# A gate vector computed on the array instead of in the network's loop, and a fixed order on ScalarE, in a two-layer diffusion trunk

## The chip, the cores and the metric

The kernel runs on one core of a Trainium2 chip. The metric is the device time of one execution in microseconds (us); lower is better. Engines are named as in the profile: PE is TensorE (matrix products and transposes), DVE is VectorE, ACT is ScalarE, SP is the queue that issues nearly all transfers.

## What is computed

Two token groups, 128 context tokens and 256 latent tokens (three blocks of 128 tokens, b = 0, 1, 2), go through two layers of one shared trunk. Cut to what matters here:

```
mod = silu(cond) @ w_mod[l] + b_mod[l]
sh1, sc1, g1, sh2, sc2, g2 = split(mod, 6)
u = layer_norm(x) * (1 + sc1) + sh1
h = mixer(u)
x = layer_norm(ALPHA * x + g1 * h)
u = layer_norm(x) * (1 + sc2) + sh2
x = layer_norm(ALPHA * x + g2 * ((silu(u @ w_gate) * (u @ w_up)) @ w_down))
```

`cond` is one vector per token group. Each of the six modulation vectors of a layer is a product of two condition vectors with a 1024 x 1024 piece of `w_mod`. Vector 5 of a layer, `g2`, is the gate of the feed-forward network ("the network" below). It is needed only when the network's output is added to `x`.

## The kernel before, in words

Weights arrive as f32 tiles of 512 KB in a ring of five buffers (tag "raw", `raw_unit`, L162). `split` (L172) makes two tiles of each: a rounded copy by ACT (L173) and the rest by DVE (L175). They go to rings of five buffers ("wr" and "wl"). A product is then three matmul passes (`in_block`, L378, and `proj`, L524).

Between the mixer and the network stands `w_out_phase`, once per layer. The string `WORDER[l]` writes out the order in which its steps are traced:

- `P b` (`project`): the output projection of block b in two halves of 512 columns, 24 matmuls each, then the residual on DVE (L358, L359), the mean (L297) and the square sum on ACT (L298, tile `junk`).
- `A b`: DVE's chain of small operations for the inverse root (L189 to L201), two DVE operations that finish x (L366), the next mean (L297) and the second square sum on ACT (L298, tile `so`).
- `B b`: the same chain, then the normalised block, by ACT (L313) for blocks 0 and 1, by DVE (L311) for block 2.
- `F b` (`to_u`, `make_u_half`): in two halves, four PE transposes (tile `puo`), four scaled copies (L330, tile `ufo`), the rounded copy on ACT (L333, tile `urf`) and the rest on DVE (L334, tile `ulf`).
- `G`, `U`: load and split two units each of the first 256 columns of `w_gate` and `w_up`.
- `H b` (`head`): the products of block b with these columns (`hg`, then `hu`), silu by ACT (L484, tile `hsg`), their product on DVE (L487), two transposes. Their banks come from a pool of two (`psA`).
- `X`: from here on DVE's part of each split is queued behind block 2's last `ulf` (`gate`). `M`: products of vectors listed in `WMODS`, which is empty.

The order of a step string is not yet the order on the engines. The framework's scheduler plays the program forward with times of its own and gives each engine what is ready, earlier traced first; `boost` raises an instruction, and `tc.issue_after(ins)` puts what is traced inside it behind `ins` on the same engine (order only, no wait for its end). The order that comes out is fixed in the program: each engine then works through its own queue.

The network (`ffn_phase`) runs over ten column pairs: gate product, silu, a piece of the down product, up product, another piece. Between them `steps` advances a generator (`all_mods`, `mod_steps`) over the vectors in `SMODS[l]`, `MSTEPS` = (3, 2) steps per pair. One step loads 512 KB of `w_mod` (tile `mraw`) and multiplies it by a column of the conditions into two row sums `z`: with ACT for the first of eight (L247), with DVE for the other seven (L250), once per condition. After eight steps 16 PE passes with a column of ones sum over partitions (L255). In layer 0 six vectors go this way, with (0, 5), the gate of layer 0's network, first; in layer 1 one.

The other way is `mod_now` with `mod_pe` (L223 to L235): each of the eight 512 KB tiles (`rawm`) goes through the "raw" ring and straight into PE against 32 columns, four products of 256 columns per tile, eight PE passes in the trace (L118 when boosted). Layer 0's mixer uses `mod_pe` for three vectors.

Of the kernel before, what the change touches and what calls it, by code (L numbers as in the profile page):

```python
# [19 lines left out]
P = 128  # L20
# [8 lines left out]
WMODS = ((), ())  # L29
TMODS = ()  # L30
SMODS = (((0, 5), (1, 1), (1, 0), (1, 3), (1, 4), (1, 2)), ((1, 5),))
# [6 lines left out]
WORDER = ("P0 P1 G A0 B0 F0 A1 B1 P2 U H0 F1 A2 B2 F2 X H1 M H2", "G P0 P1 A0 B0 A1 B1 U P2 F0 F1 H0 A2 B2 F2 X H1 M H2")  # L38
# [4 lines left out]
MSTEPS = (3, 2)  # L43
# [21 lines left out]
def trunk_kernel(ctx: ExitStack, tc: tile.TileContext, a: dict):  # L65
# [101 lines left out]
    gate = [None]  # L167

    def gated():
        return tc.issue_after(gate[0].ins) if gate[0] is not None else nullcontext()  # L170

    def split(t, r, lo):  # L172
        S.copy(r, t)  # L173
        with gated():
            V.tensor_tensor(lo, t, r, ALU.subtract)  # L175
        return r, lo
# [60 lines left out]
    def mod_steps(l, v, out):  # L237
# [3 lines left out]
        for k in range(KC):  # L241
            t = big([P, D], f"mraw{l}_{v}_{k}")
            SY.dma_start(t, w[:, k, v * D : (v + 1) * D])
            for c in range(2):
                if k == 0:
                    with gated():
                        S.mul(z[c], t, cs[:, c, k : k + 1])  # L247
                else:
                    with gated():
                        V.scalar_tensor_tensor(z[c], t, cs[:, c, k : k + 1], z[c], ALU.mult, ALU.add)  # L250
            yield k == KC - 1
# [43 lines left out]
    def acc_stats(src, junk, sums, name):  # L295
        w = perm.tile([P, 8], F32, tag="lnw", name="lnw" + name, bufs=NLNW)
        V.tensor_scalar(w[:, 0:1], sums[:, 0:1], sums[:, 1:2], -1.0 / D, ALU.add, ALU.mult)  # L297
        S.activation(junk, src, AF.Square, bias=w[:, 0:1], accum_out=w[:, 1:2])  # L298
        return w
# [6 lines left out]
    def make_xh(x, xh, w, name, fast=False):  # L306
        rs = var_rsqrt(w, name)
        nmr = w[:, 2:3]
        last = V.tensor_scalar(nmr, w[:, 0:1], rs, None, ALU.mult)
        if fast:  # L310
            V.tensor_scalar(xh, x, rs, nmr, ALU.mult, ALU.add)  # L311
        else:
            S.activation(xh, x, AF.Identity, bias=nmr, scale=rs)  # L313
        return last

    def make_u_half(b, xh, uf, sh, sc, u, bank, name, hb, fast=False):
# [4 lines left out]
        for q in range(4):  # L321
            k = hb * 4 + q
            boost(nc.tensor.transpose, pt[:, q * P : (q + 1) * P], xh[:, k * P : (k + 1) * P], ident)
# [9 lines left out]
        S.copy(ur[:, ks, cols], uf)  # L333
# [101 lines left out]
    def w_out_phase(l, pre, cat, x, gt, lnv, u2, sh2, sc2, wx, hh, bankTO, mods):  # L435
# [4 lines left out]
        units2, st = {}, {}  # L440

        def head_units(nm, src):
            v = src[l].rearrange("(k p) f -> p k f", p=P)
            units2[nm] = []
            for i in range(2):
                r, lo = split_unit(v[:, 4 * i : 4 * i + 4, 0:256], [4, 256], f"{nm}h{l}_{i}")
                units2[nm].append((r, lo, 4, 4 * i))

        def project(b):
            s = big([P, D], f"so{l}_{b}")  # L450
            sums = small([P, 2], "rsum")
            for nh in range(2):
                ps = bk("V" if (b, nh) == (1, 1) else "W", f"wo{l}_{nh}_{b}")
                in_block(ps, cat, units[nh], b, 512)
# [9 lines left out]
        def to_u(b):  # L464
            tags = iter((None, "WV", "WW")[b] or ())
            bank = bankTO if b == 0 else lambda nm: bk(next(tags), nm)
            last[b] = make_u(b, st[b][0], sh2, sc2, u2, f"o{l}_{b}", bank, b == 2)

        def mod_all():
            for ll, v in mods:  # L470
                mod_now(ll, v, bk("W", f"mw{ll}_{v}"))

        def hold_splits():
            gate[0] = last[2]

        heads = []

        def head(b):
# [5 lines left out]
            S.activation(sg, ps[:, 0:256], AF.Silu)  # L484
# [5 lines left out]
        def head_end(b, sg):  # L490
            pt = bankTO(f"ht{l}_{b}")
            for q in range(NHEAD):
# [4 lines left out]
                              "G": lambda: head_units("g", a["w_gate"]), "U": lambda: head_units("u", a["w_up"]),  # L497
                              "M": mod_all, "X": hold_splits})
# [6 lines left out]
    def ffn_phase(l, u2, x, lnp, hh, wx_es, pto, get_g, lnv, steps, keep, late, tail_units, tail_block, tail_mod, end_heads):  # L505
# [89 lines left out]
        gate[0] = None  # L595
# [37 lines left out]
        gate[0] = None  # L633
# [723 lines left out]
    for l in range(2):  # L1357
# [34 lines left out]
        end_heads = w_out_phase(l, pre, cat, x, gt, lnv, u2, m[l, 3], m[l, 4], wx, hh, bankTO, WMODS[l])  # L1392
# [135 lines left out]
```

## Time and profile before

| what | value |
|---|---|
| median of 3 runs | 1015.73 us (1014.62 to 1015.8) |
| the profiled execution's own time | 1014.2 us |
| its span in the profile | 1012.4 us |
| PE busy | 984.8 us (97%) |
| DVE busy | 667.7 us (66%) |
| ACT busy | 436.6 us (43%) |
| read from HBM | 167.52 MB, 170 GB/s over the span |
| granted PE clock | 0.998 of full speed |

The profile records one execution. The span goes from the first to the last recorded instruction; the execution's own time is 1.8 us longer. Busy time of PE counts matmuls whose ends are modelled. Idle time of an engine costs the kernel something only where the engine that bounds the stretch waits for it.

### The profile page before, as it was taken

What the parts mean: (1) busy time and instruction counts of PE and PEld (TensorE: products, weight loads), DVE (VectorE), ACT (ScalarE), POOL (GpSimd) and SP (SyncE); (2) the same over time, 40 slices, a digit from 0 to 9 for tenths busy, and PEclk for the clock granted to TensorE, in tenths of its full rate; (3) what the DMA queues carried; (4) which work ended last, traced back from release to release, by engine and by line L of the source; (5) the groups of instructions that cost most, each with busy time, mean ns of one, the idle gap of its engine ahead of it and who ended that gap; (6) DMA issues with size and microseconds to landing.
All of it is one profiled execution on the core that took longest, in us unless ns stands there. A gap on an engine that the chain in (4) does not pass through costs nothing.

```text
span 1012.4 us, 14717 instructions
## 1 busy us (share of the span) xinstructions
PE 984.8 (97%) x5583; PEld 824.2 (81%) x5583; DVE 667.7 (66%) x1368; ACT 436.6 (43%) x790; POOL 1.2 (0%) x5
## 2 busy tenths in 40 slices
PE   9999999999999999999999999999899999999996
PEld 4775567787899988989887766787799999999985
DVE  5387558588875877968788577558895333335554
ACT  3385533227533343334327555544943333333410
POOL 0000000000000000000000000000000000000000
PEclk9999999999999999999999999999999999999999
DMA  9975446473674877767754333235574544444401
GB/s 304 296 205 188 147 133 205 174 254 111 195 230 137 281 224 249 219 216 227 253 163 153 99 95 94 84 104 225 163 246 153 163 126 126 124 126 124 149 22 42
DMA packets 109704, 172.85 MB, mean 171 GB/s; under 512 B 10177, under 2 KB 78273, under 8 KB 109633
## 3 DMA queue, kind: packets, MB, share of 16 engines
q1 hardware_dynamic: 106960, 170.87, 53.0%
q10 hardware_dynamic: 2672, 1.04, 0.4%
q8 instruction: 44, 0.72, 0.3%
q14 instruction: 28, 0.22, 0.1%
HBM read 167.52 MB, written 4.36 MB: 170 GB/s over the span
## 4 chain that ended last, share of the span: by engine, by line
PE 81%; DVE 6%; ACT 6%; DMA 5%; issue 2%; SPq 0%; ACTq 0%; DVEq 0%
PE dn L544 18%; PE wg L524 15%; PE wu L524 14%; PE cd L378 7%; PE wo L378 4%; PE rvg L378 4%; PE s L378 3%; PE rqk L378 2%; PE mod L118 1%; DMA mraw<-in_w_mod 1%; DMA rawm<-in_w_mod 1%; DMA raw_wd<-in_w_down 1%; PE ms L118 1%; PE hg L378 1%; ACT ufo L330 1%
## 5 line engine op out<-in xcount | busy, mean ns | idle before, releaser
L250 DVE SCALAR_TENSOR_TENSOR z<-mraw,cs,z 128x1024 f32<-128x1024 f32 x98 | 121.5, 1281 | 12.2 <-DMA mraw<-in_w_mod 11.8
L524 PE MATMUL wu<-urf,r_wu 128*128 128x384 f32 x320 | 108.6, 340 | 1.2 <-ACT sg L565 1.2
L524 PE MATMUL wg<-urf,r_wg 128*128 128x384 f32 x320 | 108.2, 340 | 0.4 <-DVE sg L572 0.4
L524 PE MATMUL wu<-ulf,r_wu 128*128 128x384 f32 x320 | 108.3, 338 | 0.0
L524 PE MATMUL wg<-ulf,r_wg 128*128 128x384 f32 x320 | 108.2, 338 | 0.0
L524 PE MATMUL wg<-urf,l_wg 128*128 128x384 f32 x320 | 108.1, 338 | 0.0
L524 PE MATMUL wu<-urf,l_wu 128*128 128x384 f32 x320 | 108.0, 338 | 0.0
L175 DVE TENSOR_TENSOR l_wg<-raw_wg,r_wg 128x1024 fp32r<-128x1024 f32 x40 | 48.8, 1223 | 56.6 <-ACT r_wg L173 56.6
L173 ACT CAST r_wd<-raw_wd 128x1024 fp32r<-128x1024 f32 x36 | 37.8, 1050 | 94.5 <-PE wu L524 44.2
L175 DVE TENSOR_TENSOR l_wd<-raw_wd,r_wd 128x1024 fp32r<-128x1024 f32 x36 | 44.0, 1222 | 47.9 <-ACT r_wd L173 47.9
L173 ACT CAST r_wg<-raw_wg 128x1024 fp32r<-128x1024 f32 x40 | 42.0, 1050 | 74.3 <-PE dn L544 28.5
L175 DVE TENSOR_TENSOR l_wu<-raw_wu,r_wu 128x1024 fp32r<-128x1024 f32 x40 | 48.5, 1223 | 35.0 <-ACT r_wu L173 35.0
L173 ACT CAST r_wu<-raw_wu 128x1024 fp32r<-128x1024 f32 x40 | 42.0, 1050 | 57.6 <-issue 18.9
L544 PE MATMUL dn<-l_wd,hr 128*128 128x512 f32 x168 | 66.6, 396 | 0.0
L544 PE MATMUL dn<-r_wd,hr 128*128 128x512 f32 x168 | 66.5, 396 | 0.0
L544 PE MATMUL dn<-r_wd,hl 128*128 128x512 f32 x168 | 66.5, 396 | 0.0
L524 PEld LDWEIGHTS wu<-urf,r_wu 128*128 128x128 f32 x320 | 60.1, 188 | 3.6 <-ACT sg L565 2.0
L524 PEld LDWEIGHTS wg<-urf,r_wg 128*128 128x128 f32 x320 | 60.1, 188 | 2.6 <-issue 1.2
L524 PEld LDWEIGHTS wu<-ulf,r_wu 128*128 128x128 f32 x320 | 60.1, 188 | 0.5
L524 PEld LDWEIGHTS wg<-ulf,r_wg 128*128 128x128 f32 x320 | 60.1, 188 | 0.4
L524 PEld LDWEIGHTS wu<-urf,l_wu 128*128 128x128 f32 x320 | 60.1, 188 | 0.1
L524 PEld LDWEIGHTS wg<-urf,l_wg 128*128 128x128 f32 x320 | 60.1, 188 | 0.0
(415 smaller groups left out, 2163.9 us busy)
## 6 DMA issues: line engine op xcount, KB each, us to landing
mraw<-in_w_mod SPq DMA_DIRECT2D x56, 512.0 KB
raw_wd<-in_w_down SPq DMA_DIRECT2D x44, 512.0 KB
raw_wg<-in_w_gate SPq DMA_DIRECT2D x40, 512.0 KB
raw_wu<-in_w_up SPq DMA_DIRECT2D x40, 512.0 KB
rawm<-in_w_mod SPq DMA_DIRECT2D x24, 512.0 KB
raw_cd<-in_w_in_cd SPq DMA_DIRECT2D x20, 512.0 KB
ms<-in_w_mod SPq DMA_DIRECT2D x16, 512.0 KB
raw_rqk<-in_w_in_ab SPq DMA_DIRECT2D x16, 256.0 KB
```

Of the source, the lines that this page charges most:

```text
L118: return f(*args, **kw)
L173: S.copy(r, t)
L175: V.tensor_tensor(lo, t, r, ALU.subtract)
L250: V.scalar_tensor_tensor(z[c], t, cs[:, c, k : k + 1], z[c], ALU.mult, ALU.add)
L330: S.activation(uf[:, q, :], pt[:, q * P : (q + 1) * P], AF.Identity, bias=sh[:, c, k : k + 1], scale=sc[:, c, k : k + 1])
L378: op = mm(ps[:, col : col + width], u[pu][:, k0 + kk, b * P : (b + 1) * P], (r, lo)[pw][:, kk, :], start=(first and i == 0 and pu + pw == ...
L524: mm(ps[j][:, 0:NTOK], un[i][pw][:, k, j * P : (j + 1) * P], u2[pu][:, 4 * i + k, :], start=(i == 0 and k == 0 and pu + pw == 0), stop=(i ...
L544: mm(acc[b, nh], h[fc][ph][:, b * P : (b + 1) * P], wrl[pw][:, nh * 512 : (nh + 1) * 512], start=(fc == 0 and ph + pw == 0), stop=(last an ...
```

## The change

1. Vector (0, 5) leaves `SMODS[0]`, so five vectors stay in layer 0's network loop, and `MSTEPS` goes from (3, 2) to (2, 2). It is computed by `mod_now(0, 5, ...)` in step `M` of layer 0, traced between `H1` and `H2`, with a bank of the pool of two that the head blocks use.
2. `G` and `U` are traced one unit at a time. In both layers the order becomes `A0 B0 A1 B1 Y G1 U0 U1 F0 P2 F1 H0 ...` after `P0 P1`.
3. A new step `Y` records block 1's normalised copy on ACT (L313) as `gate_s`: the rounded copies of splits traced after it are queued behind it on ACT. `Y` also traces one silu of a single column, boosted, behind that copy.
4. `F0`'s ACT instructions are queued behind the last split's rounded copy traced before (that of `U1`). The second half of `P2` is queued on PE behind `F0`'s last transpose; the transposes of `F1` and `F2` behind `P2`.
5. The silu of a head block is queued behind the last `urf` copy traced before: `F1`'s for `H0`, `F2`'s for `H1`.
6. At `X`, `gate_s` becomes `F2`'s last `urf` copy: splits and the first row products of a vector (L247) traced after it are queued behind it.

```diff
-WMODS = ((), ())
-SMODS = (((0, 5), (1, 1), (1, 0), (1, 3), (1, 4), (1, 2)), ((1, 5),))
+SMODS = (((1, 1), (1, 0), (1, 3), (1, 4), (1, 2)), ((1, 5),))
...
-WORDER = ("P0 P1 G A0 B0 F0 A1 B1 P2 U H0 F1 A2 B2 F2 X H1 M H2", "G P0 P1 A0 B0 A1 B1 U P2 F0 F1 H0 A2 B2 F2 X H1 M H2")
+WORDER = ("P0 P1 G0 A0 B0 A1 B1 Y G1 U0 U1 F0 P2 F1 H0 A2 B2 F2 X H1 M H2", "G0 P0 P1 A0 B0 A1 B1 Y G1 U0 U1 F0 P2 F1 H0 A2 B2 F2 X H1 H2")
...
-MSTEPS = (3, 2)
+MSTEPS = (2, 2)
...
-    gate = [None]
-    def gated():
-        return tc.issue_after(gate[0].ins) if gate[0] is not None else nullcontext()
+    gate, gate_s = [None], [None]
+    last_s, last_split, last_t = [None], [None], [None]
+    def gated(g=gate):
+        return tc.issue_after(g[0].ins) if g[0] is not None else nullcontext()
     def split(t, r, lo):
-        S.copy(r, t)
+        with gated(gate_s):
+            last_split[0] = S.copy(r, t)
...
                 if k == 0:
-                    with gated():
+                    with gated(gate_s):
                         S.mul(z[c], t, cs[:, c, k : k + 1])
...
-            S.activation(xh, x, AF.Identity, bias=nmr, scale=rs)
+            last_s[0] = S.activation(xh, x, AF.Identity, bias=nmr, scale=rs)
...
-        S.copy(ur[:, ks, cols], uf)
+        last_s[0] = S.copy(ur[:, ks, cols], uf)
...
             for nh in range(2):
                 ps = bk("V" if (b, nh) == (1, 1) else "W", f"wo{l}_{nh}_{b}")
-                in_block(ps, cat, units[nh], b, 512)
+                with tc.issue_after(last_t[0].ins) if (b, nh) == (2, 1) else nullcontext():
+                    last_p2[0] = in_block(ps, cat, units[nh], b, 512)
...
-            last[b] = make_u(b, st[b][0], sh2, sc2, u2, f"o{l}_{b}", bank, b == 2)
-        def mod_all():
-            for ll, v in mods:
-                mod_now(ll, v, bk("W", f"mw{ll}_{v}"))
+            with tc.issue_after((last_split, last_p2, last_p2)[b][0].ins):
+                last[b] = make_u(b, st[b][0], sh2, sc2, u2, f"o{l}_{b}", bank, b == 2)
+        def gate_vector():
+            mod_now(0, 5, bankA("mw"))
+        def after_norms():
+            gate_s[0] = last_s[0]
+            tiny = small([P, 1], "silu")
+            with gated(gate_s):
+                boost(S.activation, tiny, ones[:, 0:1], AF.Silu)
         def hold_splits():
             gate[0] = last[2]
+            gate_s[0] = last_s[0]
...
-            S.activation(sg, ps[:, 0:256], AF.Silu)
+            with tc.issue_after(last_s[0].ins):
+                S.activation(sg, ps[:, 0:256], AF.Silu)
...
-        gate[0] = None
+        gate[0] = gate_s[0] = None
```

## Rows read from the trace of the kernel before

**Rows 1.** The page's first part: busy us, share of the span, instructions of each engine

```profile
PE 984.8 (97%) x5583; PEld 824.2 (81%) x5583; DVE 667.7 (66%) x1368; ACT 436.6 (43%) x790; POOL 1.2 (0%) x5
```

**Rows 2.** Windows, core 0: PE, PEld, DVE, ACT, POOL busy; granted clock; DMA share; GB/s

```profile
243.00:269.00 26.00, 22.13 (x170) 20.38 (x169) 20.03 (x56) 20.42 (x40) 0.00 (x0) 1.00 0.45 141
269.00:480.00 211.00, 211.00 (x1154) 194.92 (x1153) 163.58 (x168) 77.37 (x93) 0.00 (x0) 1.00 0.71 227
480.00:530.00 50.00, 48.13 (x268) 42.38 (x268) 42.26 (x62) 15.81 (x21) 0.00 (x0) 1.00 0.65 205
712.00:741.00 29.00, 26.15 (x194) 24.02 (x193) 24.34 (x62) 24.84 (x46) 0.00 (x0) 1.00 0.49 156
```

**Rows 3.** Timeline of PE: start, length, instruction, [idle before it <- what ended that]

```profile
516.40 1.07 PE L255 MATMUL mod<-z,ones 128*32 128x256 f32 x16 [0.69 <-DVE sg L572]
717.88 0.38 PE L378 MATMUL hg<-r_gh,ulf 128*128 128x256 f32 x1 [0.93 <-DVE ulf L334]
726.33 0.39 PE L378 MATMUL hg<-r_gh,urf 128*128 128x256 f32 x1 [1.35 <-ACT hsg L484]
```

**Rows 4.** Timeline of ACT, layer 0, around head block 0

```profile
247.65 2.21 ACT L247 ACTIVATE z<-mraw,cs 128x1024 f32<-128x1024 f32 x2
249.88 1.28 ACT L484 ACT_TABLE_LOAD   x1
251.17 0.38 ACT L484 ACTIVATE hsg<-hg 128x256 f32<-128x256 f32 x1
```

**Rows 5.** Chain that ended last, in order of time, layer 1: projection, last head block, network

```profile
693.95 10.49 PE wo L378 x45
737.32 2.85 PE hu L378 x24
740.17 8.45 PE wg L524 x48
```

**Rows 6.** Timeline of DVE, layer 1: residual, mean, one chain, finishing x

```profile
700.43 0.75 DVE L366 SCALAR_TENSOR_TENSOR x<-x,lnwao,lnv 128x512 f32<-128x512 f32 x1
704.46 0.69 DVE L358 TENSOR_TENSOR so<-wo,g 128x512 f32<-128x512 f32 x1 [2.59 <-PE wo L378]
705.91 0.21 DVE L297 TENSOR_SCALAR lnwao<-rsum 128x1 f32<-128x1 f32 x1
717.14 0.68 DVE L334 TENSOR_TENSOR ulf<-ufo,urf 128x512 fp32r<-128x512 f32 x1
727.96 0.15 DVE L189 TENSOR_SCALAR lnwbo<-lnwbo 128x1 f32<-128x1 f32 x1 [0.45 <-ACT so L298]
729.48 0.81 DVE L311 TENSOR_SCALAR so<-x,lnwbo 128x1024 f32<-128x1024 f32 x1
```

**Rows 7.** Timeline of ACT, layer 1, from block 1's square sum to `F0`

```profile
706.57 1.15 ACT L298 ACTIVATE junk<-so,lnwao 128x1024 bf16<-128x1024 f32 x1
708.85 1.99 ACT L173 CAST r_uh<-raw_uh 128x1024 fp32r<-128x1024 f32 x2
711.78 1.25 ACT L313 ACTIVATE so<-x,lnwbo 128x1024 f32<-128x1024 f32 x1
714.06 1.83 ACT L330 ACTIVATE ufo<-puo,modc,modc 128x128 f32<-128x128 f32 x5
715.78 0.62 ACT L333 CAST urf<-ufo 128x512 fp32r<-128x512 f32 x1
```

**Rows 8.** Timeline of PE: eight transposes; two tiles of a vector by `mod_pe` back to back

```profile
718.22 1.04 PE L118 MATMUL puo<-ident,so 128*128 128x128 f32 x8
90.82 1.18 PE L118 MATMUL mod<-rawm,cmod 128*32 128x256 f32 x16
```

**Rows 9.** Timeline of SP, layer 0: the last tile loaded ahead of the head blocks

```profile
222.59 0.38 SPq L164 DMA_DIRECT2D raw_wg<-in_w_gate  x1
```

**Rows 10.** Groups by line: the row products on DVE

```profile
L250 DVE SCALAR_TENSOR_TENSOR z<-mraw,cs,z 128x1024 f32<-128x1024 f32 x98 | 121.5, 1281 | 12.2 <-DMA mraw<-in_w_mod 11.8
```

**Rows 11.** Windows, the last stretch, columns as in rows 2

```profile
1005.00:1012.00 7.00, 0.00 (x0) 0.00 (x0) 4.08 (x15) 1.24 (x2) 0.00 (x0) 0.68 0.20 75
```

More of the change, by code (lines that the diff above doesn't have):

```diff
@@ L297, in acc_stats @@
         V.tensor_scalar(w[:, 0:1], sums[:, 0:1], sums[:, 1:2], -1.0 / D, ALU.add, ALU.mult)
-        S.activation(junk, src, AF.Square, bias=w[:, 0:1], accum_out=w[:, 1:2])
+        last_s[0] = S.activation(junk, src, AF.Square, bias=w[:, 0:1], accum_out=w[:, 1:2])
         return w
@@ L322, in make_u_half @@
             k = hb * 4 + q
-            boost(nc.tensor.transpose, pt[:, q * P : (q + 1) * P], xh[:, k * P : (k + 1) * P], ident)
+            last_t[0] = boost(nc.tensor.transpose, pt[:, q * P : (q + 1) * P], xh[:, k * P : (k + 1) * P], ident)
         for q in range(4):
@@ L433, in wo_unit, with w_out_phase @@
         return r, lo, 2, 2 * i
-    def w_out_phase(l, pre, cat, x, gt, lnv, u2, sh2, sc2, wx, hh, bankTO, mods):
+    def w_out_phase(l, pre, cat, x, gt, lnv, u2, sh2, sc2, wx, hh, bankTO):
         bk = Banks(f"pw{l}", W=3, V=1)
@@ L439, in w_out_phase, with head_unit @@
         units[1] = pre + [wo_unit(l, 1, i, extra_rl(wx, nx, f"{l}{i}")) for i in KORDER[l][len(pre) :]]
-        units2, st = {}, {}
-        def head_units(nm, src):
+        units2, st, last_p2 = {}, {}, [None]
+        def head_unit(nm, src, i):
             v = src[l].rearrange("(k p) f -> p k f", p=P)
[L444 to L447, printed above, removed]
+            r, lo = split_unit(v[:, 4 * i : 4 * i + 4, 0:256], [4, 256], f"{nm}h{l}_{i}")
+            units2.setdefault(nm, []).append((r, lo, 4, 4 * i))
         def project(b):
@@ L496, in w_out_phase @@
         run_order(WORDER[l], {"P": project, "A": norm, "B": norm, "F": to_u, "H": head,
-                              "G": lambda: head_units("g", a["w_gate"]), "U": lambda: head_units("u", a["w_up"]),
-                              "M": mod_all, "X": hold_splits})
+                              "G": lambda i: head_unit("g", a["w_gate"], i), "U": lambda i: head_unit("u", a["w_up"], i),
+                              "Y": after_norms, "M": gate_vector, "X": hold_splits})
         bk.close()
@@ L632, in ffn_phase @@
                 keep(b, x[b])
-        gate[0] = None
+        gate[0] = gate_s[0] = None
         accp.close()
@@ L1391, in trunk_kernel @@
         hh = tuple(lnp.tile([P, NHEAD, NTOK], F32R, name=f"hh{q}{l}") for q in "rl")
-        end_heads = w_out_phase(l, pre, cat, x, gt, lnv, u2, m[l, 3], m[l, 4], wx, hh, bankTO, WMODS[l])
+        end_heads = w_out_phase(l, pre, cat, x, gt, lnv, u2, m[l, 3], m[l, 4], wx, hh, bankTO)
         if wxr_es is not None:
```

## The prediction, made before the changed kernel ran

> **What bounds the kernel now.** I read the page's busy times first [rows 1]: PE is busy for 984.8 us of a span of 1012.4 us. A change can therefore gain by two things only, fewer PE passes or less of the 27.6 us in which PE is idle. The windows say where idle time lies in the stretches that the change touches [rows 2]. Between the projections and the network PE is idle for 26 - 22.13 = 3.87 us in layer 0 and 29 - 26.15 = 2.85 us in layer 1. In layer 0's network, 269 to 480 us, it is never idle, though DVE works there for 163.58 of 211 us: taking work off DVE, ACT or the transfers in that stretch gains nothing. At the network's end, 480 to 530 us, 1.87 us are idle.
>
> The idle gaps one by one [rows 3]: in layer 1 head block 0 waits 0.93 us for DVE's `ulf` of block 0, and block 1 waits 1.35 us for the silu that empties a bank; at the end of layer 0's network the last vector's passes wait 0.69 us for DVE to empty a bank. ACT's timeline shows why block 1 is late in layer 0 [rows 4]: 2.21 us of row products for the vector and the load of the silu table stand between block 0's and block 1's copies.
>
> **The order, in layer 1, where nothing else changes.** Time runs from 704.46 us, where DVE takes up block 1's last product. Today head block 0 gets going at 717.88 us, 13.4 us later [rows 3], and the network starts at 740.17, 35.7 us later [rows 5].
>
> In the new order, `F0`'s copies stand on ACT behind three split copies, and those behind block 1's normalised copy. The chain to head block 0 is then, from [rows 4, 6, 7]: residual and mean 1.7 (704.46 to 705.91, and 0.21); square sum 1.15; chain of small operations 1.5 (727.96 to 729.48); two operations that finish x 1.4; mean 0.2; second square sum 1.15; chain 1.5; normalised copy 1.25; table load 1.3 (249.88 to 251.17); the one-column silu, which no row shows, 0.2 (between 0 and the 0.38 of a 256-column one); three split copies 3.0 (two take 1.99); four `ufo` copies and `urf` 2.1 (five take 1.83, `urf` 0.62, they overlap); `ulf` 0.7. Sum 17.1 us. If block 0's copy (1.25) and chain (1.5) cut in fully, 19.9; I take the lower sum, since ACT waits for DVE twice in this chain and can do block 0's copy meanwhile.
>
> PE has for this time block 2's 48 projection matmuls, 11.2 us (45 take 10.49 [rows 5]), and the transposes of blocks 0 and 1, 1.04 each [rows 8]: 13.3 us. It waits 3.8 us where it waited 0.93.
>
> After that, things get better. From 717.88 to 740.17 are 22.3 us, 1.92 of them idle (2.85 - 0.93), and block 1's transposes (1.04) now lie in the wait: 19.3 us of work remain. One new wait appears: the silu of block 0 is queued behind `F1`, so its bank comes free after `F0`'s second half (2.1), block 2's square sum (1.15), `F1` (4.2) and itself (0.4), 7.85 us after `F0`'s first half, while PE needs 0.7 (`ulf`) and 5.7 us (twice the 2.85 of 24 matmuls [rows 5]): 1.4 us. New total 17.1 + 19.3 + 1.4 = 37.8 against 35.7: **+2.1 us**. Bounds: -2.85 if every idle microsecond goes, +4.9 with the 19.9.
>
> What this moves besides: the row products (1.15 each on ACT) and the split copies for the network wait until `F2` is done. Behind them come two split copies and two DVE operations, about 4 us, under head block 2's 5.7 us of PE: no cost, and if that cover fails up to 2 us.
>
> **The order in layer 0.** The same steps, and the stretch today has 1.0 us more idle time (3.87 against 2.85), so the same new order costs 2.1 - 1.0 = **+1.1 us** (bounds -3.9 and +3.9).
>
> **The gate vector on PE.** Two tiles back to back take 1.18 us [rows 8], so eight take 8 x 0.59 = 4.7 us. How much falls into waits the trace of before does not show. From below: all but 0.9 us fits into the new wait of 3.8. From above: all of it stands in line, and three of its eight tiles have to be loaded through the ring of five after the first have been used: 512 KB at 227 GB/s [rows 2] are 2.3 us each, 6.9 us, less the 3.0 us that the first five tiles' passes take, so 4.7 + 3.9 = 8.6 us. SP had a buffer free as early as 222.59 us [rows 9], so some tiles are there before the wait; with four of eight in it (2.4 us) the vector costs **+2.3 us**. On SP its eight transfers now stand ahead of the network's first units; those are needed only after head block 2, so I cost that at nothing within these bounds.
>
> **What the network loses.** The old vector's 16 passes over the row sums, **-1.1 us** (1.07 [rows 3]). The 14 products on DVE, 18 us at 1281 ns [rows 10], and 4 MB of loads: nothing, PE was never idle beside them. At the end fewer steps are left, so the bank should be emptied in time: **-0.7 us** (bounds 0 and -0.7). Steps per column pair fall from five to four and steps in all from 48 to 40, so the last vector still ends with the last pair. Layer 1's eight steps only spread over more pairs.
>
> **Sum:** 2.1 + 1.1 + 2.3 - 1.1 - 0.7 = **+3.7 us**. The profiled execution took 1014.2 us and becomes 1017.9; it lies 1.5 us below the median of the runs, so for the median I give 1015.7 + 3.7 = 1019.4 us. About 0.2% (2 us) is what a measurement of this kernel can tell from no change.
>
> A word on the table. In the trace the load takes 1.28 us and the silu starts 1.29 us after the load began [rows 4]. The Trainium skill, page "ScalarE: Activation LUTs", section "What ACT_TABLE_LOAD costs", counts about 1.38 us of drain on top, 2.66 us per switch. By that figure, an estimate, each layer's chain would be 1.4 us longer and the sum +6.5 us. The trace does not show a drain here, and the measurement decides.
>
> **Rivals.**
>
> *The order pays.* Row products, one split copy and the table load leave the space between blocks 0 and 1 [rows 4, 7], and these caused most of today's gaps. If the scheduler lets block 0 and block 1 run through ACT more tightly than my chain, so that `F0` is done when block 2's second projection half ends, about two thirds of the 6.7 us of waits go: -4.5, with 4.7 - 1.1 - 0.7 = 2.9 for the vector, 1.2 of it in the waits left: -2.8 us, 1012.9 us. It decides at 14 us after 704.46. For it: ACT is full in the stretch, 24.84 of 29 us [rows 2]. Against it: my chain has three split copies and the table load where today `F0` stands.
>
> *It evens out.* The vector's passes are scheduled ahead of head block 0 and nearly fill the wait (1.2 us left), and the order costs 1.1 us in layer 1 and nothing in layer 0: +0.5 us, 1016.2 us. The diff puts the vector between head blocks, but the scheduler may do otherwise, as with the interleaved steps of the mixer.
>
> *The vector stands in line.* Its bank comes from the pool of two and is free only when block 1's silu, queued behind `F2`, has emptied it, and half of the ring's 3.9 us is added: 6.6 instead of 2.3 us, +8.0 us, 1023.7 us.
>
> *The clock falls.* In the last stretch PE does nothing and the granted clock is 0.68 on average [rows 11], so part of it at 1.2 instead of 2.4 GHz; in all windows of [rows 2] it is 1.00. My new wait of 3.8 us is longer than any gap there. If it drops the clock, head block 0's 5.7 us double in each layer: +3.7 + 11.4, 1030.8 us. The Trainium skill, page "TensorE: Matmul & The Clock Gate", section "Why this matters for your kernels", warns of idle gaps between bursts of matmuls for this reason; by that rule this rival would be the likely one. But block 2's second half parts the wait in two, so I leave it a small chance.
>
> **How the numbers follow.** Forecast 0.42 (own range 1017.6 to 1022, by the bounds of the chain and the vector); the order pays 0.24; it evens out 0.20; the vector stands in line 0.10; the clock falls 0.04. Faster than 1013.7: nearly all of the second case and a little of the third, 0.26. Within 0.2%: most of the third and the low edge of the forecast, 0.21. Slower: 0.53. The range 1012.5 to 1025.0 leaves out the clock, the far ends of the first and fourth case, and a general doubt, 0.2 together.
>
> **What would show it.** Right: PE idle 3 to 6 us before head block 0 in layer 1, ended by `ulf` or `urf`, with three split copies and a table load on ACT just before `F0`; a short wait before head block 1 ended by `hsg`; eight groups of `rawm` passes near the head blocks of layer 0; no 16 passes at the network's start; no gap at its last vector. Wrong: head block 0 of layer 1 starting less than 14 us after DVE's residual, or the network of layer 1 starting earlier than 35.7 us after it.

## The result, and the profile after

The changed kernel takes 1031.34 us (median of four runs, 1030.03 to 1033.31); the kernel before, run beside it, 1015.76 (1014.62 to 1016.81). The ratio is 1.0155, with a 95% interval of 1.0135 to 1.0175: slower by some 15.7 us. The forecast of 1019.4 had the sign; the size lies far outside its range. The profiled execution took 1031.72 us with a span of 1029.9, 17.5 us more than before.

Two kinds of marks in the timelines cut the span into stretches: DVE taking up block 1's last residual product (231.99 before and 232.19 after in layer 0, 704.46 and 716.07 in layer 1), and the first gate product `wg` of each network. (In layer 1 of the kernel before that product starts at 740.00 by the timeline; the chain's group, which the prediction used, starts at 740.17.)

| stretch | before | after | change |
|---|---|---|---|
| start to layer 0's residual | 232.0 | 232.2 | +0.2 |
| layer 0: residual to network | 36.9 | 46.5 | +9.6 |
| layer 0's network to layer 1's residual | 435.6 | 437.4 | +1.8 |
| layer 1: residual to network | 35.5 | 41.7 | +6.2 |
| layer 1's network to the end | 272.4 | 272.1 | -0.3 |

First the page's busy times of the changed kernel, as [rows 1], then its windows over the same work as [rows 2] (PE, PEld, DVE, ACT, POOL busy; granted clock; DMA share; GB/s).

```profile
PE 992.8 (96%) x5631; PEld 830.0 (81%) x5631; DVE 652.4 (63%) x1353; ACT 435.5 (42%) x790; POOL 1.2 (0%) x5
```

```profile
243.00:275.00 32.00, 27.89 (x221) 23.39 (x219) 17.16 (x45) 20.39 (x42) 0.00 (x0) 0.96 0.48 164
480.00:530.00 50.00, 47.27 (x278) 43.20 (x277) 38.20 (x43) 19.92 (x25) 0.00 (x0) 1.00 0.68 216
712.00:745.00 33.00, 29.23 (x164) 25.43 (x163) 23.24 (x82) 21.28 (x39) 0.00 (x0) 0.90 0.25 77
```

DVE lost 15 us, PE gained 8, and PE's clock is below 1.00 in both stretches between projection and network, where it was 1.00. The idle rows of PE, where [rows 3] had waits of 0.69, 0.93 and 1.35:

```profile
241.51 1.14 PE L117 MATMUL puo<-ident,so 128*128 128x128 f32 x8 [3.76 <-ACT so L315]
265.58 2.37 PE L231 MATMUL mw<-rawm,cmod 128*32 128x256 f32 x40 [1.85 <-ACT hsg L494]
270.57 0.64 PE L231 MATMUL mw<-rawm,cmod 128*32 128x256 f32 x8 [1.00 <-DMA rawm<-in_w_mod]
273.27 0.64 PE L231 MATMUL mw<-rawm,cmod 128*32 128x256 f32 x8 [0.80 <-DMA rawm<-in_w_mod]
289.09 0.44 PE L534 MATMUL wu<-urf,r_wu 128*128 128x384 f32 x1 [1.57 <-ACT r_wu L175]
...
725.38 1.97 PE L117 MATMUL puo<-ident,so 128*128 128x128 f32 x8 [3.77 <-ACT so L315]
750.25 0.38 PE L380 MATMUL hg<-r_gh,urf 128*128 128x256 f32 x1 [1.85 <-ACT hsg L494]
```

In each layer PE stands still for 3.76 or 3.77 us ahead of `F0`'s transposes, until ACT has block 0's normalised copy, with block 2's second projection half queued behind them. Another 1.85 us pass until block 1's silu, queued behind `F2` on ACT, has emptied a bank. In layer 0 the vector then waits twice for its tiles, and the first up product for a split copy. The windows around the first wait in each layer, and one behind layer 1's second wait, show what follows:

```profile
240.00:242.00 2.00, 0.49 (x4) 0.49 (x5) 1.19 (x9) 1.78 (x2) 0.00 (x0) 1.00 0.00 0
242.00:244.00 2.00, 2.00 (x10) 1.72 (x9) 0.00 (x0) 1.97 (x3) 0.00 (x0) 0.60 0.01 4
244.00:246.00 2.00, 2.00 (x6) 1.54 (x6) 0.85 (x1) 2.00 (x4) 0.00 (x0) 0.54 0.00 0
246.00:248.00 2.00, 2.00 (x11) 1.63 (x10) 2.00 (x3) 2.00 (x6) 0.00 (x0) 1.00 0.38 49
...
724.00:726.00 2.00, 0.61 (x3) 0.62 (x4) 1.06 (x8) 1.91 (x2) 0.00 (x0) 0.50 0.00 0
726.00:728.00 2.00, 2.00 (x9) 1.81 (x8) 0.00 (x0) 1.97 (x4) 0.00 (x0) 0.50 0.00 0
728.00:730.00 2.00, 2.00 (x6) 1.60 (x5) 0.98 (x1) 2.00 (x4) 0.00 (x0) 0.50 0.00 0
...
752.00:754.00 2.00, 2.00 (x11) 2.00 (x11) 0.92 (x2) 1.79 (x3) 0.00 (x0) 0.50 0.24 39
```

The granted clock falls to 0.50, the level of 1.2 GHz; 0.60 and 0.54 are means over windows in which it stood at 1.00 for a part. The projection's matmuls start 0.43 us apart there (243.30, 243.73) and 0.23 apart at 1.00 (246.32, 246.55). In layer 1 the clock falls a second time, behind the wait of 1.85 us, and is back at 1.00 from 755 us on. ACT's timeline of layer 0 (as [rows 4], with the steps that the chain of the prediction counted) shows why `so` is late:

```profile
235.11 1.14 ACT L300 ACTIVATE so<-x,lnwbo 128x1024 f32<-128x1024 f32 x1
...
238.41 1.15 ACT L300 ACTIVATE so<-x,lnwbo 128x1024 f32<-128x1024 f32 x1 [2.07 <-issue]
...
240.22 2.45 ACT L315 ACTIVATE so<-x,lnwbo 128x1024 f32<-128x1024 f32 x2 [0.56 <-DVE lnwbo L311]
242.68 1.28 ACT L117 ACT_TABLE_LOAD   x1
243.98 0.20 ACT L117 ACTIVATE silu<-ones 128x1 f32<-128x1 f32 x1
244.09 1.03 ACT L175 CAST r_gh<-raw_gh 128x1024 fp32r<-128x1024 f32 x1
245.02 1.99 ACT L175 CAST r_uh<-raw_uh 128x1024 fp32r<-128x1024 f32 x2
```

Both normalised copies (x2 at 240.22) stand behind block 1's second square sum of 238.41, though block 0's own had ended two microseconds before that one began (235.11 + 1.14). But ACT waits another 0.56 us after that square sum, for DVE: these are the first and the last operation of block 0's second chain.

```profile
236.40 0.15 DVE L191 TENSOR_SCALAR lnwbo<-lnwbo 128x1 f32<-128x1 f32 x1
...
239.91 0.21 DVE L311 TENSOR_SCALAR lnwbo<-lnwbo 128x1 f32<-128x1 f32 x1
```

The chain takes 3.7 us where 1.5 was counted, because DVE does the finishing of block 1 and the first half of block 2's residual between its steps. Last, SP's timeline of layer 0, its order around the vector:

```profile
266.28 1.28 SPq L163 DMA_DIRECT2D rawm<-in_w_mod  x3
267.65 1.35 SPq L163 DMA_DIRECT2D raw_wg<-in_w_gate  x2
276.65 2.31 SPq L288 DMA_DIRECT2D gs<-bm  x8
279.06 0.36 SPq L163 DMA_DIRECT2D raw_wd<-in_w_down  x1
...
279.99 0.93 SPq L163 DMA_DIRECT2D raw_wu<-in_w_up  x2
```

Three tiles of the vector are loaded only once PE has begun on the first, at 265.58. The eight stores of the result (`gs`) wait for DVE's sum, and the loads that the network needs next wait behind them. That does not make these loads the last cause of PE's 1.57 us before `wu`. ACT's rows there:

```profile
287.34 0.49 ACT L575 ACTIVATE sg<-wg 128x384 f32<-128x384 f32 x1 [1.63 <-PE wg L534]
...
287.98 2.00 ACT L175 CAST r_wu<-raw_wu 128x1024 fp32r<-128x1024 f32 x2
```

The copies of `raw_wu` start with no wait for a transfer. They are queued behind a silu for which ACT stood idle for 1.63 us.

### The profile page after: what moved, and what is told of

It is laid out like the page before. It is cut to its first block, busy times and chain, and to the rows that moved or that the text cites. A ratio compares the mean times of both kernels' runs of the same rounds, so it can differ in the third digit from the quotient of the medians.

```text
span 1029.9 us, 14794 instructions
## 1 busy us (share of the span) xinstructions
PE 992.8 (96%) x5631; PEld 830.0 (81%) x5631; DVE 652.4 (63%) x1353; ACT 435.5 (42%) x790; POOL 1.2 (0%) x5
## 4 chain that ended last, share of the span: by engine, by line
PE 60%; DVE 6%; DMA 3%; ACT 3%; issue 1%; SPq 0%; ACTq 0%; DVEq 0%
PE dn L554 17%; PE wu L534 15%; PE wg L534 15%; PE cd L380 7%; PE wo L380 3%; DMA mraw<-in_w_mod 2%; DVE z L252 1%; DMA raw_wd<-in_w_down 1%; ACT dp L1244 1%; DMA rawm<-in_w_mod 1%; PE hu L380 1%; DVE x L368 1%; ACT ufd L332 1%; DVE x L342 1%; PE mod L257 1%
## 5 line engine op out<-in xcount | busy, mean ns | idle before, releaser
L252 DVE SCALAR_TENSOR_TENSOR z<-mraw,cs,z 128x1024 f32<-128x1024 f32 x84 | 104.1, 1281 | 5.6 <-DMA mraw<-in_w_mod 5.2
L175 ACT CAST r_wd<-raw_wd 128x1024 fp32r<-128x1024 f32 x36 | 37.8, 1050 | 95.0 <-PE wg L534 47.4
```

Of the source, the lines that this page charges most:

```text
L175: last_split[0] = S.copy(r, t)
```

## The experiments

Each run is compared with the kernel before on the same chip; 0.1% are 1.0 us.

**Run 1: the vector back in the network.**

```diff
-SMODS = (((1, 1), (1, 0), ...
+SMODS = (((0, 5), (1, 1), (1, 0), ...
-MSTEPS = (2, 2)
+MSTEPS = (3, 2)
-... F2 X H1 M H2", "G0 ...
+... F2 X H1 H2", "G0 ...
```

> The changed kernel with vector (0, 5) back in the network's loop (six vectors, steps 3 and 2, no step M in layer 0); the order of the steps stays as changed. Theory: layer 0 lost 11.5 us (9.5 before its network, 2.0 in and after it), layer 1, which has no such vector, 6.0; the difference of 5.5 us is the vector's, so about 1026 us (1024.5 to 1027.5), layer 0's network start about 43 us after block 1's residual, and no wait before wu. Rival, the vector fills waits that are there anyway and layer 0's order is just worse than layer 1's: less than 2 us gained, 1029.5 or more.

Measured 1024.30 us, ratio 1.0087 (1.0064 to 1.0111): 0.68% less than the changed kernel, 6.9 us. Layer 0's network starts 40.9 us after the residual, layer 1's still 41.7. The vector costs some 7 us: by the marks 5.6 ahead of layer 0's network and 1.2 between it and layer 1's residual (436.2 instead of 437.4). The rest is in both layers alike. The wait of 1.85 us stays (now before head block 2), so it is not the vector's.

**Run 2: the vector alone, in the kernel before.**

```diff
-WMODS = ((), ())
+WMODS = (((0, 5),), ())
-SMODS = (((0, 5), (1, 1), ...
+SMODS = (((1, 1), ...
-MSTEPS = (3, 2)
+MSTEPS = (2, 2)
-                mod_now(ll, v, bk("W", f"mw{ll}_{v}"))
+                mod_now(ll, v, bankA("mw"))
```

> The kernel before with the vector alone moved to the array between head blocks 1 and 2 (bank from the pool of two, steps 2 and 2); nothing of the order is changed. Theory: as in the first run, about +5.5 us against the kernel before, 1021 us (1019.5 to 1022.5), with a wait for the tiles that must be loaded through the ring of five and one before wu. Rival of the prediction, 16 passes fewer and waits filled: +1 us or less, 1017.

Measured 1021.04 us, 1.0050 (1.0036 to 1.0065): +5.1 us, as the theory had it; layer 0's network starts 42.0 us after the residual instead of 36.9. The wait for a tile is there (0.87 us), the one before `wu` is not, though SP's stores stand ahead of `raw_wu` here too: ACT has the first copy of it between two silus. Ten runs lie between 1017.77 and 1023.29, and the profiled one shows a place that may spread them: in the mixer of layer 1 ACT's split of a head unit stands ahead of the copy of the mixer's output and waits for its transfer, and PE waits for that. First ACT, then PE of this run:

```profile
682.96 1.05 ACT L173 CAST r_gh<-raw_gh 128x1024 fp32r<-128x1024 f32 x1 [3.62 <-DMA raw_gh<-in_w_gate]
```

```profile
685.27 0.44 PE L118 MATMUL dot<-ident,do 128*128 128x128 f32 x2 [2.07 <-DVE catl L393]
```

In the kernel before the same split waits 1.77 us, and no gap of PE over 0.31 us follows there.

**Run 3: block 2's second half no longer behind `F0`.**

```diff
-                with tc.issue_after(last_t[0].ins) if (b, nh) == (2, 1) else nullcontext():
+                with nullcontext():
                     last_p2[0] = in_block(ps, cat, units[nh], b, 512)
```

> The changed kernel without the rule that queues block 2's second projection half behind F0's transposes; the scheduler then sets 16 of its 24 matmuls ahead of them. Theory: PE's single wait of 3.76 us shrinks to about 0.1 in both layers and the granted clock stays at 1.00 there: 2 x 3.7 us of wait and 1.7 (layer 0) and 3.3 us (layer 1) of clock go, about -12 us, 1019 (1017 to 1022). Rival: the chain through ACT and DVE sets the time, the wait only moves to head block 0; then only the clock's part or nothing comes back, -5 us at most, 1026 or more.

Measured 1025.63 us, 1.0095 (1.0073 to 1.0118). The rival was right: the wait moves to head block 0, at full length, and takes the fall of the clock with it. PE's row (layer 0) and the windows behind it:

```profile
248.62 0.58 PE L380 MATMUL hg<-r_gh,urf 128*128 128x256 f32 x1 [4.00 <-ACT urf L335]
```

```profile
248.00:250.00 2.00, 1.33 (x4) 1.04 (x5) 1.96 (x6) 2.00 (x6) 0.00 (x0) 0.50 0.99 360
250.00:252.00 2.00, 2.00 (x12) 2.00 (x11) 1.88 (x8) 2.00 (x6) 0.00 (x0) 0.50 0.71 277
```

Head block 0 starts 17.1 us after the residual in both layers: ACT's and DVE's chain sets that, whatever PE does meanwhile. This run too has the stores ahead of `raw_wu` on SP and no wait before `wu`; its row on ACT, to be held against that of the changed kernel at 287.98, starts right behind the first silu:

```profile
284.01 1.04 ACT L175 CAST r_wu<-raw_wu 128x1024 fp32r<-128x1024 f32 x1
```

**Run 4: the wait filled.** 14 matmuls that nobody reads stand in the wait.

```diff
+        def fill_wait():
+            project(2, (0,))
+            ps = bankA(f"fill{l}")
+            for i in range(14):
+                with tc.issue_after(last_p2[0].ins):
+                    last_p2[0] = boost(mm, ps, cat[0][:, 0, P : 2 * P], units[1][0][0][:, 0, :], start=True, stop=True)
...
-... U0 U1 F0 P2 ...
+... U0 U1 Q F0 P2 ...
...
-            in_block(ps, u2, units2["g"], b, 256)
+            hg_last = in_block(ps, u2, units2["g"], b, 256)
...
-            in_block(ps, u2, units2["u"], b, 256)
+            with tc.issue_after(hg_last.ins):
+                in_block(ps, u2, units2["u"], b, 256)
```

> The changed kernel with 14 matmuls of 512 columns whose results nobody reads, about 3 us, in PE's wait of 3.76 us before F0's transposes, in both layers (up products also queued behind gate products, so the heads' order stays). The wait's length is not changed by them. Theory that the drop of the clock costs time by itself: granted clock 1.00 from there on, block 2's second half at 0.23 us a matmul instead of 0.43, -1.7 us in layer 0, -3.3 and up to -1.7 (second drop) in layer 1: about -6, 1025.5 (1024 to 1027.5). Rival, the slow clock is hidden behind the copies that head block 0 waits for: within 1 us of 1031.3.

Measured 1025.85 us, 1.0104 (1.0082 to 1.0126): 5.2 us less than the changed kernel by the ratios, for work that does nothing. `F0` is no earlier; the clock stays. PE's row and the windows behind it in layer 0:

```profile
243.51 1.09 PE L117 MATMUL puo<-ident,so 128*128 128x128 f32 x8 [0.55 <-ACT so L315]
```

```profile
244.00:246.00 2.00, 2.00 (x13) 1.74 (x12) 0.00 (x0) 1.97 (x3) 0.00 (x0) 1.00 0.01 4
246.00:248.00 2.00, 2.00 (x10) 1.65 (x10) 0.85 (x1) 2.00 (x4) 0.00 (x0) 1.00 0.00 0
```

Layer 1's network starts 37.9 us after the residual instead of 41.7. One thing besides the clock differs: `F2`'s transposes came to stand ahead of head block 1's up products, not behind 15 of them, and the waits of 1.85 us are gone. Runs 13 and 14 take that apart.

**Run 5: a shorter chain.** As run 3, and two of the three split copies leave ACT's row ahead of `F0`.

```diff
-... Y G1 U0 U1 F0 P2 ...
+... Y G1 F0 U0 U1 P2 ...
...
                 last[b] = make_u(b, st[b][0], sh2, sc2, u2, f"o{l}_{b}", bank, b == 2)
+            if b == 0:
+                gate_s[0] = last_s[0]
```

> As the third run (block 2's second half free), and in both layers F0 is traced ahead of U0 and U1, whose split copies are queued behind F0's last rounded copy on ACT: two of the three split copies, 2.0 us, leave the chain to head block 0. Theory: the chain is ACT's row of copies, so head block 0 starts 15.1 instead of 17.1 us after block 1's residual, PE's wait before it falls from 4.0 to 2.0 us, and whether the granted clock then falls decides the rest: 1021.5 if it does, about 1016 if it stays at 1.00 (range 1014.5 to 1023). Rival, the chain is DVE's small operations and not ACT's copies: head block 0 stays at 17, 1025.6.

Measured 1028.06 us, 1.0119 (1.0105 to 1.0133), above the range. The chain itself came out as worked out: head block 0 starts 15.2 us after the residual in both layers, its wait is 2.10 us, with a second one of 0.87 just behind it. But that was enough for the clock:

```profile
247.13 0.39 PE L380 MATMUL hg<-r_gh,urf 128*128 128x256 f32 x1 [2.10 <-ACT urf L335]
248.39 0.57 PE L380 MATMUL hg<-r_gh,ulf 128*128 128x256 f32 x1 [0.87 <-DVE ulf L336]
```

```profile
248.00:250.00 2.00, 1.61 (x7) 1.61 (x8) 1.63 (x7) 2.00 (x5) 0.00 (x0) 0.61 0.50 203
250.00:252.00 2.00, 2.00 (x12) 2.00 (x11) 1.97 (x6) 2.00 (x4) 0.00 (x0) 0.54 0.04 8
```

Both networks start earlier than in run 3 (44.2 and 37.7 us after the residual against 45.2 and 38.2), so where the time went is not here. The profiled execution lost 1.9 us against run 3 in the stretch that holds the network and the mixer of layer 0 to 1 (439.9 against 438.0), and the mixer's end shows the wait of run 2 again (1.71 us). That explains the profiled run only in part; the rest of the gap to the range stays open.

**Run 6: the vector's stores on POOL.**

```diff
-                SY.dma_start(sc[cnd, j : j + 1, :], mp[32 * j + cnd : 32 * j + cnd + 1, :])
+                (G if name == "0_5" else SY).dma_start(sc[cnd, j : j + 1, :], mp[32 * j + cnd : 32 * j + cnd + 1, :])
```

> The changed kernel, with the eight stores of the gate vector's result issued from POOL instead of SP. In the changed kernel SP waits 7.6 us at them for DVE's sum, and two weight loads of the network stand behind them; PE then waits 1.57 us for a split copy. Theory: that wait goes, -1.6 us, 1029.8 (1028.8 to 1030.5), rest as it was. Rival, the weights are late because eight more tiles went through the ring ahead of them: no difference, 1031.3.

`raw_wu` is issued at 276.88 instead of 279.99, in an execution that is 2.9 us late at that point, and PE's wait before `wu` is gone. But ACT's order changed with it: both copies of `raw_wu` now stand ahead of the first silu (283.90 and 285.35, the silu at 288.10). So the earlier loads are shown, and that the stores made the wait of 1.57 us is not. The time is inconclusive: 1030.48 us, 1.0131 (1.0109 to 1.0152), four runs from 1026.04 to 1035.26.

**Runs 7 and 8: the early table and the late row products, in the kernel before.** Run 7 has both edits, run 8 the first alone.

```diff
             next(st[b][1])
+            if b == 0:
+                tiny = small([P, 1], "silu")
+                with tc.issue_after(last_s[0].ins):
+                    boost(S.activation, tiny, ones[:, 0:1], AF.Silu)
...
-                    with gated():
+                    with tc.issue_after(gate_z[0].ins) if gate_z[0] is not None else nullcontext():
                         S.mul(z[c], t, cs[:, c, k : k + 1])
...
             gate[0] = last[2]
+            gate_z[0] = last_ur[0]
```

Here `last_s` is the last square sum and `last_ur` the last `urf` copy.

> The kernel before with only two of the ideas: a silu of one column behind block 0's first square sum, so that the table is loaded before the chain, and the first row products of a vector (2 x 1.1 us) queued behind F2's last copy on ACT. The vector stays in the network, nothing else is gated. Theory: PE's waits between the head blocks (1.3 us in layer 0, 1.35 in layer 1) were made by these 3.5 us on ACT, and they go: about -2.5 us, 1013 (1011.5 to 1014.5). Rival: they were made by the copies' own length; no difference, 1015.5.

> The kernel before with the early silu alone. Theory: 1.28 us of 3.5 on ACT between blocks 0 and 1: about -1 us, 1014.5 (1013.5 to 1015.5). Rival: the table load stood in time that ACT had left, no difference; or the load in its new place delays block 1's copies, +0.5.

Run 7: 1011.22 us, 0.9956 (0.9944 to 0.9968), 4.5 us faster than the kernel before and the best against it. Run 8: 1012.01 us, 0.9968 (0.9958 to 0.9978). The table load is most of it by the medians, though the two intervals overlap, and both gained more than was expected. Run 8's networks start 1.2 and 1.4 us earlier after the residual, about one table load (1.28) in each layer. ACT's rows of run 7 in layer 0, and the windows that answer to the first and last of [rows 2]:

```profile
225.75 1.28 ACT L118 ACT_TABLE_LOAD   x1
...
249.04 0.38 ACT L490 ACTIVATE hsg<-hg 128x256 f32<-128x256 f32 x1 [1.54 <-PE hg L379]
...
260.62 2.19 ACT L248 ACTIVATE z<-mraw,cs 128x1024 f32<-128x1024 f32 x2
```

```profile
240.00:266.00 26.00, 23.63 (x178) 21.68 (x178) 20.49 (x59) 21.23 (x44) 0.00 (x0) 1.00 0.41 123
710.00:737.00 27.00, 25.89 (x191) 23.70 (x191) 23.30 (x67) 23.82 (x46) 0.00 (x0) 1.00 0.47 149
```

PE's idle time falls from 3.87 to 2.37 us in layer 0 and from 2.85 to 1.11 in layer 1, and the networks start 1.6 and 2.1 us earlier after the residual than in the kernel before.

**Runs 9 and 12: the vector ahead of the wait.** Run 12 adds the stores on POOL, as in run 6.

```diff
-"P0 P1 G0 A0 B0 A1 B1 Y G1 U0 U1 F0 P2 F1 H0 A2 B2 F2 X H1 M H2"
+"P0 P1 M G0 A0 B0 A1 B1 Y G1 U0 U1 F0 P2 F1 H0 A2 B2 F2 X H1 H2"
```

> The changed kernel with step M traced right behind P1 instead of between H1 and H2; nothing else is moved. The vector's passes (4.3 us) then stand between block 1's and block 2's projection, ahead of the wait of 3.76 us. Theory: they are useful work in that wait, so in layer 0 the wait and the fall of the clock go, the waits for tiles between the head blocks too, and layer 0's network starts 39 to 41 us after block 1's residual instead of 46.5; layer 1 is unchanged: about 1025 (1023 to 1027). Rival, the tiles pass the ring of five ahead of the head units, and r_gh then comes late: head block 0 waits, 1029 or more.

> The ninth kernel (step M right behind P1) with the stores of its result on POOL, as in the sixth. In the ninth run SP's stores, waiting for DVE's sum until 239.87, held back the two raw_uh loads behind them, ACT waited 2.00 us for one, and F0's copies stand behind that split. Theory: SP loads raw_uh right behind raw_gh, head block 0 of layer 0 starts 17 to 18 us after block 1's residual instead of 20.0, its waits of 2.11 and 2.35 us shrink below 1.5 together, the granted clock stays at 1.00 in layer 0, and layer 0's network starts 39 to 40.5 us after the residual instead of 43.7; layer 1 is unchanged: 1020.5 (1019 to 1022.5). Rival, raw_uh waits for buffers of the ring and not for SP's stores: 1024, as in the ninth run.

Run 9: 1024.11 us, 1.0091 (1.0074 to 1.0109), the expected time, but by another way. The wait ahead of `F0` is gone, a new one stands at head block 0, and the clock falls there. PE, then ACT and SP:

```profile
250.77 0.39 PE L380 MATMUL hg<-r_gh,urf 128*128 128x256 f32 x1 [2.11 <-ACT urf L335]
253.62 0.58 PE L380 MATMUL hg<-r_gh,ulf 128*128 128x256 f32 x1 [2.35 <-DVE ulf L336]
```

```profile
246.35 2.11 ACT L175 CAST r_uh<-raw_uh 128x1024 fp32r<-128x1024 f32 x2 [2.00 <-DMA raw_uh<-in_w_up]
```

```profile
239.87 2.31 SPq L288 DMA_DIRECT2D gs<-bm  x8
242.28 0.94 SPq L163 DMA_DIRECT2D raw_uh<-in_w_up  x2
```

Run 12: 1021.38 us, 1.0056 (1.0038 to 1.0074). SP issues `raw_uh` from 235.43 on, head block 0 starts 17.9 us after the residual, the clock is 1.00 in every window of layer 0 from 240 to 256 us, and the network starts after 38.7 us instead of 46.5. That is 0.8 us more than without the vector and with the clock held (run 10, 37.9). So the price hangs on the vector's place and on its stores: behind `P1` most of its passes fill the wait, and they hold the clock there as well. (PE's order within the head blocks differs between runs 9 and 12 too, so what lies between their times is not the stores' wait alone.)

**Run 10: the order alone, with the clock held.** Runs 1 and 4 together.

> The changed order alone with the clock held: vector back in the network as in the first run, and 14 unread matmuls in PE's wait as in the fourth. Theory, the three causes add up: order 2.4 us in each layer, no vector, no fall of the clock: about 1015.5 + 5 = 1020.5 (1018.5 to 1022), both networks 38 us after the residual. Rival, clock and vector are one cause: 1024, as in the first run.

Measured 1017.74 us, 1.0028 (1.0009 to 1.0047), below the expected range; both networks start 37.9 us after the residual, 1.0 and 2.4 us later than in the kernel before.

**Run 11: run 7 with layer 1's `G` behind `P1`.**

```diff
-"G P0 P1 A0 B0 A1 B1 U P2 ...
+"P0 P1 G A0 B0 A1 B1 U P2 ...
```

> The early table and late products as in the seventh run, and layer 1's first head units (G) traced behind P1 instead of ahead of P0. In profiles with a long mixer, the split copy r_gh stands on ACT ahead of a copy of the mixer's output and waits up to 3.6 us for its transfer; PE then waits up to 2.1 us. Theory: the wait goes for good, runs lie closer together and the median falls by 0.5 to 1.5 us to about 1010.3 (1009.5 to 1011.5). Rival: the transfer is late because the queue is full, and another copy waits in its place: 1011.2 and the same spread.

Measured 1010.51 us, 0.9961 (0.9948 to 0.9974). Run 7's profile still had 0.66 us of that wait at the mixer's end, this one has none, but ratio and spread (1009.76 to 1011.24) are those of run 7 (1010.71 to 1011.92): no gain that can be told.

**Runs 13 and 14: `F2`'s transposes early, without filling.** Run 13 on the changed kernel, run 14 on run 1.

```diff
-            in_block(ps, u2, units2["g"], b, 256)
+            hg_last = in_block(ps, u2, units2["g"], b, 256)
...
-            in_block(ps, u2, units2["u"], b, 256)
+            with tc.issue_after((last_t[0] if b == 1 else hg_last).ins):
+                in_block(ps, u2, units2["u"], b, 256)
```

> The changed kernel with one rule more, no filling: head block 1's up products are queued behind F2's transposes on PE (in the changed kernel these stand behind 15 of the 24). That is the place they had in the fourth and tenth runs, whose gain over the changed kernel can therefore be the clock's or F2's place. If F2's place made the wait of 1.85 us (the bank that head block 1's silu frees, queued behind F2): that wait goes in both layers, and with it the second fall of the clock in layer 1, about -3.5 us, 1028 (1026.5 to 1029.5), head block 0 still 18 and 19 us after the residual. If the clock made it all: no change, 1031.3.

> The same rule, with the vector back in the network as in the first run; against the tenth run only the unread matmuls are missing, so the difference is the clock's alone (with the first fall in each layer). By the starts of head block 0, 1.0 us later in layer 0 and 1.9 in layer 1 than with filling: 1018.5 + 3 = 1021.5 (1020 to 1023). If all of the 6 us between the first and the tenth run were the clock's: 1024.3.

Run 13: 1028.87 us, 1.0144 (1.0127 to 1.0160). Run 14: 1022.37 us, 1.0070 (1.0053 to 1.0086). Here `last_t` is the last transpose traced so far, `F2`'s when `b` is 1. The wait of 1.85 us does not go, it changes its name: block 2's projection ends late, so its normalised copy does, and PE's row in run 13 is

```profile
259.99 1.09 PE L117 MATMUL puo<-ident,so 128*128 128x128 f32 x8 [1.97 <-DVE so L313]
```

With the clock held (run 4) the same row waits 0.29 us. From run 14 to run 10 are 0.42%, 4.3 us; the starts of the networks move by 2.7 and 3.5 us (40.6 and 41.4 to 37.9). PE has the same order in both but for the filling. On ACT and DVE the scheduler set a few instructions behind `F0` in another order (block 2's first square sum comes earlier), and that is a rival to the clock. The timelines rule it out:

| from the timelines, layers 0 and 1 | changed kernel | run 14 | run 10 |
|---|---|---|---|
| `F0`'s first transpose to the end of block 2's projection | 8.2, 9.1 | 8.2, 9.1 | 6.6, 6.7 |
| from there to the end of block 2's normalised copy | 11.8, 11.8 | 11.8, 11.8 | 11.9, 11.8 |

The slow projection alone delays block 2's copy, by 1.6 and 2.4 us, and the second wait, of 1.85 or 1.97 us, comes from that. So the clock's share is 4 (by the ratios) to 6 us (by the marks). `F2`'s place moves the ratio by 0.17% (runs 1 and 14) and 0.11% (changed kernel and run 13), both within the intervals.

## Why the prediction was right in sign and wrong in size

The runs split the 15.7 us by ratios: the order with the clock held 2.8 (run 10), the fall of the clock and the late `F2` behind it 6.0 (run 1 less run 10), the vector 6.9 (all less run 1). Each ratio is known to about 2 us, and the parts depend on each other: the vector alone costs 5.1 (run 2) and, with the clock held, 7.7 (run 4 less run 10).

**The order: right.** It was priced at 2.1 in layer 1 and 1.1 in layer 0; with the clock held the networks start 2.4 and 1.0 us later. The total of 37.8 us for layer 1 stands against 37.9. Adding up a chain from single rows of another order worked, but not every term did. Head block 0 starts 17.1 us after the residual in runs 3, 4 and 10; that is its first product, which needs `urf` alone. The predicted 17.1 ended with `ulf`, and the first product with `ulf` starts after 17.9 us (run 10, both layers). Against that, the new wait of 1.4 us ended by `hsg` is not in run 10. Two errors of about a microsecond cancel in the total. The trace shows no drain at the table load either: the small silu begins 1.30 us after the load began (242.68 to 243.98), as in [rows 4]. The 1.38 us that the Trainium skill, page "ScalarE: Activation LUTs", section "What ACT_TABLE_LOAD costs", adds as a drain do not appear here.

**The clock: the step that failed.** The prediction knew the wait (3.8 us, measured 3.76) and the risk, and dismissed it with "block 2's second half parts the wait in two". Two things were wrong. It also said that ACT "can do block 0's copy meanwhile"; ACT did stand idle (2.07 us), but the copy came behind block 1's second square sum and behind DVE's mixed chain. So `F0`'s transposes, with the second half behind them by the change's own rule, waited in one piece, and the sign "PE idle 3 to 6 us before head block 0" did not come. Freeing the second half does not save it: in run 3 the same wait stands in one piece at head block 0, and in run 5, where it is shorter and in two pieces (2.10 and 0.87 us), the clock falls too. The price, 11.4 us, was too high against 4 to 6, and laid on the wrong work: not head block 0 ran at the low clock but block 2's second half, for some 3.5 us in layer 0 and 5 in layer 1, and in layer 1 the last head block for 3.5 more. That the sum with this price, 1030.8, lies beside the measured 1031.34 is luck: it holds 5 to 7 us too much for the clock and some 6 too little for the vector. The Trainium skill, page "TensorE: Matmul & The Clock Gate", section "Why this matters for your kernels", warns of idle gaps between bursts; the trace agrees, a clock of 0.50 after 3.76 us of idle time against 1.00 after [rows 3]'s gaps, but it also fell after 1.85 us. By that warning the prediction had called this rival the likely one, and it gave it 0.04.

**The vector: mis-sized.** It was priced at +2.3 on PE, -1.1 for the old passes and -0.7 at the network's end, +0.5 in all; it is 6.9. None of its tiles fell into the long wait, since PE's queue has them behind head block 1; run 12, which puts them ahead, gets most of the time back. Its passes took 2.37 for five tiles and 0.64 for each of three, 4.3 us, near the 4.7 estimated. Then come waits that the prediction bounded but did not take: 1.8 us for tiles through the ring, 0.25 behind them (a bank), and 1.57 us before `wu`. The last was missed outright. The prediction put the transfers on SP at nothing, with the tiles in mind, while eight stores that wait for DVE stood ahead of the network's loads. These stores do hold loads back: in the order of run 9 that costs ACT 2.00 us, and run 12 takes it away. For the 1.57 us here the row on ACT shows another last cause, the place of the `raw_wu` copies behind a silu, and runs 2 and 3 have the stores without the wait. Less the 1.07 us of old passes all this makes 6.85; that it meets the 6.9 of the ratios so closely is chance, with 2 us on each. The rival "the vector stands in line" had 6.6 us, before the old passes come off (7.9 here), and gave the bank as the reason; the bank's wait of 1.85 us is there without the vector too (run 1).

**The network's end: wrong by a little.** PE's gaps from 480 us to the mixer's first `cd` product sum to 2.73 us (0.67, 1.21, 0.85), against 1.86 before (0.78, 0.39, 0.69): the -0.7 did not come. The gap at the last vector's passes is still there, 0.85 us instead of 0.69. In run 1, with the vector back, the gaps sum to 2.70, so the number of steps in the loop is not what sets them. Between 291 and 480 us PE is never idle, as before, so that DVE does 14 products fewer there gains nothing, as predicted.

**The new wait** of 1.4 us came as 1.85, one block later, behind block 1's silu instead of block 0's. It follows from the slow projection, as the table under runs 13 and 14 shows.

The rivals were set out as ways that exclude each other, and the range followed from that. Here two came together with the forecast: 2.8 for the order, the clock's 4 to 6, the vector's 7.

## What to carry to other kernels

A wait of the engine that bounds the kernel is priced twice, by its length and by the slower clock behind it; where its end can't be moved, put useful work in it (run 12), or at least any work (run 4). A step that is moved takes its stores with it: on SP's queue, which worked in order here, a store that waits for a sum held back the loads behind it (runs 9 and 12). A wait belongs to the row that ended it: before `wu` the late loads stood out, and the order on ACT ended the wait. And causes that can happen together are added up in the range, not weighed against each other.

## What was not expected of the hardware

- The clock fell after 2.10 us of idle time with 0.87 us more just behind it (run 5: 0.61, then 0.54), as after one of 3.76 us. After single waits of 1.85 to 1.98 us it fell in some places (layer 1 of the changed kernel, both layers of run 14) and stayed at 1.00 in others (layer 0 of the changed kernel, both layers of run 13). It stayed at 1.00 with 0.34, 0.34 and 0.57 us in a row (run 4), and in the kernel before with 0.98 and 0.35.
- After waits of equal length (3.76 and 3.77) the fall did not last equally long: in layer 0 the clock was back at 1.00 from 246 us on, in layer 1 it stood at 0.50 from 724 to 730 us, and had begun to fall while PE still waited (0.85 in the window of 723 to 724).
- Eight stores of 1 KB took SP 2.31 us to issue and POOL 3.95 us.
- The same transfer of `raw_gh` in the mixer of layer 1 ended ACT's wait after 1.38 us in one profile and 3.62 in another; in the kernel before it was 1.77. The kernel before ran from 1010.88 to 1018.20 us over all measurements here; whether this transfer is the reason is not shown, since one execution of it was profiled.
